# Embedding products in the token selection, and another order for the first expert pair, in an fp32 two-block decoder

## The chip, the cores and the metric

One core of one Trainium2 chip runs the whole program in one launch. The time is in device microseconds (us), the median of three runs. Names: PE is the matrix engine (TensorE; PEld its weight loads), DVE the vector engine, ACT the scalar engine, POOL the general one (GpSimd); SP issues every DMA here and issues them in the order of its queue.

## What is computed

The inputs are one sequence of 512 tokens with 1024 channels, all fp32. A first block (a recurrent mixer, sparse attention, two gated convolution FFNs) is followed by a second one of two layers. Each of these layers has four mixer branches, then an expert-choice MoE with 16 experts, then a gated embedding; the change is in the last two:

```
affinity = softmax((h @ w_router), axis=-1)                  # h = rms_norm(x, g_moe[i])
top_aff, idx = top_k(swapaxes(affinity, 1, 2), 64)           # each expert takes its 64 best tokens
xe = h[idx]
hid = silu(xe @ w_gate_e) * (xe @ w_up_e)                    # 1024 -> 1024, for each expert
ye = hid @ w_down_e
x = x + scatter_add(idx, ye * top_aff)
x = x + sigmoid(rms_norm(x, g_ple[i]) @ w_ple_gate[i]) * (p[i] @ w_ple[i])
```

The products p[i] @ w_ple[i] need no result of the layer: p is an input of 512 tokens by 256 channels, the result has 1024 channels by 512 tokens (2.1 MB).

## The kernel before, in words

Activations stand with channels on the 128 partitions: hT is 8 tiles of [128, 512]. Dense products split both operands into a rounded part and a rest (xh, xl; wh, wl) and take three matmuls per 128x128 block (L408 to L410). Dense weights come as a stream of 512 KB chunks of eight blocks (class Stream): a load into one of four wraw buffers, a rounded copy on ACT (wh), a subtraction on DVE (wl), each into a pool of three buffers.

**The experts** are worked on in eight pairs. Their weights are not split: 384 chunks of 512 KB a layer, 32 for the two up products of a pair and 16 for its down product, each used once by pairmm (L1884: two fp32 matmuls, one per expert, 64 tokens each, which the trace shows as four records). `expert_chunks` is a generator that issues the loads: chunk i goes into the next free buffer, and `chunk()` hands the chunks to PE in the order of the list `order`. There are 36 buffers to begin with: a ring of 21 (11 of its own, the four wraw buffers, three wh and three wl) that is refilled as PE gives buffers back, and 15 that are lent by tiles which are needed only later (hid, yh, yl, hidT, D, xe, sqt, xd) and hold one chunk each, once. `extra` says which chunks go to the lent ones: numbers 2, 5, 8, ... 44. The first loads are issued by `prefetch` in the output projection (`mixer_out`), the rest at the head of `moe`.

**The selection** (the first half of `moe`): PE transposes the router's logits, DVE and ACT make the softmax, PE transposes it to 16 rows of 512 tokens, and DVE takes eight rounds of the eight largest and their replacement (L1839, L1840). A scan counts the chosen tokens along each row (L1844), PE transposes the counts, and DVE compares them with 1 to 64, which gives the one-hot matrix D (L1855). Beside it PE transposes the hidden state, ACT scales and rounds it (xn, xh, L1832, L1833) and POOL makes the rest (L1834).

**The experts' loop:** `gather(q)` picks the tokens of four experts by matmuls with D (L1866, L1867; four steps of 16 matmuls, each giving two of the eight channel tiles of xe). The first one is a generator: `up(0, ahead)` runs a step of it ahead of every second chunk. Then, for p = 0 to 7: up(p + 1); gather(p/2 + 1) when p is even; in the last two rounds also half of the embedding products (`ple_proj`, eight outputs of two blocks, results kept in SBUF as pb); down(p), which combines two pairs into hT when p is odd.

The builder's scheduler orders each engine's instructions by their dependences; what stands in a row is quoted below from the built program.

Of the kernel before, what the change touches and what calls it, by code (L numbers as in the profile page):

```python
# [19 lines left out]
P = 128  # L20
# [172 lines left out]
class Stream:  # L193
    def __init__(self, kb, n_chunks):
        self.kb, self.nch, self.specs, self.pos, self.next, self.ahead = kb, n_chunks, [], CHB, 0, []
        self.pool = False
# [9 lines left out]
    def open(self):  # L206
        kb = self.kb
        if not self.ahead:
            self.preload()
        raw = self.ahead.pop(0)  # L210
        self.h = kb.wsp.tile([P, CHB, P], F32R, name="wh")
        self.l = kb.wsp.tile([P, CHB, P], F32R, name="wl")
        kb.nc.scalar.activation(self.h, raw, AF.Copy)  # L213
        (kb.nc.gpsimd if self.pool else kb.nc.vector).tensor_sub(self.l, raw, self.h.bitcast(F32))  # L214
        self.pos = 0
# [37 lines left out]
class Kern:  # L253
# [773 lines left out]
    def build(self, only2=False):  # L1027
# [18 lines left out]
        with ExitStack() as es:  # L1046
# [3 lines left out]
            for l in range(2):  # L1050
                with ExitStack() as es2:
# [16 lines left out]
                    with ExitStack() as es4:  # L1068
# [5 lines left out]
                        with ExitStack() as es3:  # L1074
                            self.psum_pools(es3, psum)
                            self.mixer_out(l)
                            self.ws.flush()
# [139 lines left out]
    def mixer_out(self, l):  # L1217
# [17 lines left out]
        for d in range(KD):  # L1235
# [12 lines left out]
            self.prefetch(2)  # L1248
        self.stats1()
        route(KD - 1)  # L1250
        self.lg = self.mo2.tile([NE, S], F32, name="lg", tag="sg")
        nc.scalar.activation(self.lg, lg[:NE], AF.Copy)

    def expert_chunks(self, l):
# [3 lines left out]
        order = up(0)  # L1258
# [3 lines left out]

        def ep():
            return self.eraw.tile([P, 2, S], F32, name="eraw")

        def lent():
            for pl, tag, k in ((self.mo2, "hid", 2), (self.mo3, "yh", 3), (self.mo3, "yl", 3), (self.mo1, "hidT", 1),
                               (self.mo2, "D", 1)):
                for _ in range(k):
                    yield pl.tile([P, 2, S], F32, name="raw", tag=tag)  # L1270
            two = self.mid.tile([P, 4, S], F32, name="raw", tag="xe")
            yield two[:, 0:2]
            yield two[:, 2:4]

        def stream():
            for _ in range(4):
                yield self.wraw.tile([P, 2, S], F32, name="wraw")
            for nm in ("wh", "wl"):
                for _ in range(3):
                    yield self.wsp.tile([P, 2, S], F32, name="raw", tag=nm)  # L1280
# [6 lines left out]
        extra = [2 + 3 * j for j in range(15)]  # L1287
        rest = iter([i for i in range(len(order)) if i not in extra])
        for _ in range(NEX):
            load(next(rest), ep())  # L1290
            yield
        for i, raw in zip(extra, lent()):
            load(i, raw)
            yield
        for raw in stream():
            load(next(rest), raw)
            yield
        load(extra[12], self.sqt)
        yield
        for i in extra[13:]:  # L1300
            load(i, self.mo2.tile([P, 2, S], F32, name="raw", tag="xd"))
            yield
        while True:
            for g in ((ep() for _ in range(NEX)), stream()):
                for raw in g:
                    i = next(rest, None)
                    if i is None:
                        return
                    load(i, raw)
                    yield  # L1310
# [481 lines left out]
    def moe(self, l):  # L1792
        nc = self.nc
        keep, two, three = self.mo1, self.mo2, self.mo3
        if True:
            self.prefetch(23 + NEX - len(self.eready))
            posm = self.sq[:NE]
            pT = keep.tile([P, T, NE], F32, name="pT")
            aff = keep.tile([P, T, NE], F32, name="aff")
            bc = lambda a: a[:, :, None].to_broadcast([P, T, NE])  # L1800
            t3 = lambda a: a.rearrange("p (t e) -> p t e", t=T)

            pt = self.pst.tile([P, S], F32, name="t")
# [10 lines left out]
            nc.vector.tensor_tensor(out=aff, in0=aff, in1=bc(sm), op=OP.mult)  # L1814
            pt = self.pst.tile([P, S], F32, name="t")
# [5 lines left out]
            xnh = self.xh.rearrange("p k s -> p (k s)").rearrange("p (t c) -> p t c", t=T)  # L1821
            xnl = self.xl.rearrange("p k s -> p (k s)").rearrange("p (t c) -> p t c", t=T)
            for t in range(T):
                xn = two.tile([P, 2, S], F32, name="xn", tag="xd")
                for hf in range(2):
                    pt = self.mm.tile([P, S], F32, name="mm")
                    for q in range(4):
                        nc.tensor.transpose(pt[:, q * P:(q + 1) * P], self.hT[:, hf * 4 + q, t * P:(t + 1) * P],
                                            self.ident)
                    sl = slice(hf * S, (hf + 1) * S)  # L1830
# [233 lines left out]
```

## Time and profile before

| | us |
|---|---|
| median of 3 runs (lowest, highest) | 3582.73 (3582.24, 3585.94) |
| the profiled execution, its own time | 3584.79 |
| its span | 3583.0 |
| PE busy | 3446.6 (96%) |
| DVE, ACT, POOL busy | 1720.5, 1259.5, 460.5 |
| mean DMA rate over the span | 173 GB/s |

The profiled execution is one run; 1.8 us of its time lie outside the span, and it is 2.1 us above the median. Matmuls overlap in PE's pipeline, so a record is longer than the time to the next one, and a busy PE is not one at its peak. The two MoE stages lie at about 1934 to 2450 and 3009 to 3525 us of the span.

### The profile page before, as it was taken

The page shows a single profiled execution, that of the slowest core. Times are in us where ns is not written, and L with a number is a line of the kernel's source. Part 1 is how long each engine was busy: PE and PEld are TensorE (multiplying, and loading weights), DVE is VectorE, ACT ScalarE, POOL GpSimd, SP SyncE. Part 2 cuts the span into 40 slices and gives each one's busy share as a digit, 9 for nine tenths or more (in the row PEclk, how much of TensorE's full clock was granted, in tenths as well). Part 3 has the DMA queues.
Part 4 walks back from the last instruction along what each step waited for, and adds up shares of the span by engine and source line. Part 5 has one row for each costly group of instructions (what it writes and reads, how often), then busy time and mean ns, then how long its engine had stood idle before and what let it go on. Part 6 is the DMA issues. An engine that isn't in the chain of part 4 may idle for free.

```text
span 3583.0 us, 42155 instructions
## 1 busy us (share of the span) xinstructions
PE 3446.6 (96%) x16156; PEld 2332.3 (65%) x16156; DVE 1720.5 (48%) x3181; ACT 1259.5 (35%) x2207; POOL 460.5 (13%) x356
## 2 busy tenths in 40 slices
PE   7899999999999999999997999999999997999997
PEld 5787888866578888876885433337876885433335
DVE  7745354477765354766664111016666664111015
ACT  5533233366643234435533100014435533100013
POOL 4211011022021012110012000002110012000002
PEclk9999999999999999999999999999999999999999
DMA  3233322311022223221253899994221253999993
GB/s 116 82 107 124 99 95 97 114 39 39 19 83 94 100 95 112 77 71 59 86 189 135 354 419 419 420 391 160 77 71 59 86 188 135 351 419 419 419 391 117
DMA packets 171474, 620.54 MB, mean 173 GB/s; under 512 B 19332, under 2 KB 19588, under 8 KB 171016
## 3 DMA queue, kind: packets, MB, share of 16 engines
q1 hardware_dynamic: 171272, 617.84, 46.0%
q8 instruction: 127, 2.08, 0.2%
q14 instruction: 75, 0.61, 0.1%
HBM read 613.82 MB, written 3.95 MB: 172 GB/s over the span
## 4 chain that ended last, share of the span: by engine, by line
PE 82%; DVE 9%; DMA 4%; ACT 2%; issue 1%; POOL 1%; DVEq 0%; SPq 0%; ACTq 0%; POOLq 0%
PE mm L408 15%; PE mm L409 15%; PE mm L410 15%; PE mm L1884 10%; PE o L1884 5%; DMA eraw<-in_exw 2%; PE o L856 1%; DMA raw<-in_exw 1%; PE mm L1866 1%; PE t L840 1%; DVE wl L214 1%; PE mm L1867 1%; PE o L1585 1%; DVE xl L326 1%; PE o L1724 1%
## 5 line engine op out<-in xcount | busy, mean ns | idle before, releaser
L408 PE MATMUL mm<-xh,wh 128*128 128x512 f32 (+1 forms) x1936 | 767.8, 397 | 6.2 <-DVE mu L1173 4.7
L410 PE MATMUL mm<-xh,wl 128*128 128x512 f32 (+1 forms) x1936 | 761.8, 394 | 2.9 <-DVE wl L214 2.3
L409 PE MATMUL mm<-xl,wh 128*128 128x512 f32 (+1 forms) x1936 | 761.5, 393 | 0.0
L214 DVE TENSOR_TENSOR wl<-wraw,wh 128x1024 fp32r<-128x1024 f32 x356 | 446.3, 1254 | 382.0 <-ACT wh L213 376.6
L213 ACT ACTIVATE wh<-wraw 128x1024 fp32r<-128x1024 f32 x378 | 399.8, 1058 | 585.0 <-PE mm L409 417.8
L408 PEld LDWEIGHTS mm<-xh,wh 128*128 128x128 f32 (+1 forms) x1936 | 364.0, 188 | 94.8 <-issue 6.8
L410 PEld LDWEIGHTS mm<-xh,wl 128*128 128x128 f32 (+1 forms) x1936 | 363.7, 188 | 86.4 <-issue 5.8
L409 PEld LDWEIGHTS mm<-xl,wh 128*128 128x128 f32 (+1 forms) x1936 | 363.9, 188 | 82.2 <-issue 8.2
L341 POOL TENSOR_TENSOR sq<-sq,sqt 128x512 f32<-128x512 f32 x63 | 90.7, 1439 | 1284.3 <-ACT sqt L338 1276.9
L1884 PE MATMUL mm<-eraw,xe 128*64 128x512 f32 x1024 | 248.1, 598 | 1.0 <-DMA eraw<-in_exw 0.9
L1900 DVE TENSOR_TENSOR hid<-sg,mm 128x512 f32<-128x512 f32 x32 | 22.0, 687 | 380.6 <-PE mm L1884 365.9
L1884 PE MATMUL mm<-raw,xe 128*64 128x512 f32 x640 | 159.6, 600 | 1.7 <-DMA raw<-in_exw 1.3
L1884 PEld LDWEIGHTS mm<-eraw,xe 128*64 128x64 f32 x1024 | 70.9, 137 | 136.8 <-issue 108.4
L579 POOL TENSOR_TENSOR fc<-fc,RB 128x512 f32<-128x512 f32 x48 | 85.4, 1779 | 575.7 <-ACT fc L578 575.7
L410 PE MATMUL mm<-gh,wl 128*128 128x512 f32 x384 | 149.5, 389 | 0.0
L408 PE MATMUL mm<-gh,wh 128*128 128x512 f32 x384 | 149.5, 389 | 0.0
L409 PE MATMUL mm<-gl,wh 128*128 128x512 f32 x384 | 149.5, 389 | 0.0
L1174 POOL TENSOR_TENSOR mg<-mg,mu 128x512 f32<-128x512 f32 x48 | 69.5, 1449 | 563.3 <-DVE mu L1173 517.2
L1884 PE MATMUL o<-eraw,hidT 128*64 128x512 f32 x560 | 138.1, 601 | 2.0 <-DMA eraw<-in_exw 0.9
L1899 ACT ACTIVATE sg<-mm 128x512 f32<-128x512 f32 x32 | 19.1, 597 | 312.4 <-PE mm L1884 312.4
L1926 ACT ACTIVATE yh<-o,af 128x512 fp32r<-128x512 f32 x32 | 22.0, 687 | 293.6 <-PE o L1884 293.4
L1927 DVE SCALAR_TENSOR_TENSOR yl<-o,af,yh 128x512 fp32r<-128x512 f32 x32 | 24.0, 750 | 189.3 <-ACT yh L1926 189.1
(492 smaller groups left out, 5704.8 us busy)
## 6 DMA issues: line engine op xcount, KB each, us to landing
eraw<-in_exw SPq DMA_DIRECT2D x396, 512.0 KB, 9.9
wraw<-in_wst SPq DMA_DIRECT2D x378, 512.0 KB, 3.3
raw<-in_exw SPq DMA_DIRECT2D x232, 512.0 KB, 9.9
wraw<-in_exw SPq DMA_DIRECT2D x138, 512.0 KB, 9.9
tb<-t5d SPq DMA_DIRECT2D x8, 448.0 KB, 3.4
mixt<-in_mix SPq DMA_DIRECT2D x2, 1344.0 KB, 6.3
hT<-in_xT SPq DMA_DIRECT2D x8, 256.0 KB, 6.0
out_dram<-po SPq DMA_DIRECT2D x8, 256.0 KB, 2.3
```

Source lines behind the costliest of these rows:

```text
L213: kb.nc.scalar.activation(self.h, raw, AF.Copy)
L214: (kb.nc.gpsimd if self.pool else kb.nc.vector).tensor_sub(self.l, raw, self.h.bitcast(F32))
L326: nc.vector.scalar_tensor_tensor(self.xl[:, k, :], h, g, self.xh[:, k, :].bitcast(F32), op0=OP.mult, op1=OP.subtract)
L341: nc.gpsimd.tensor_add(acc, acc, t)
L408: nc.tensor.matmul(out, a, h, start=(k == 0), stop=False)
L409: nc.tensor.matmul(out, a, l, start=False, stop=False)
L410: nc.tensor.matmul(out, b, h, start=False, stop=(k == n - 1))
L579: nc.gpsimd.tensor_mul(c0, c0, self.RB)
L840: nc.tensor.transpose(pt[:, r * P:(r + 1) * P], srcs(i, r), self.ident)
L856: nc.tensor.matmul(o[0][c % 2 * HD:(c % 2 + 1) * HD], lhs(i), pe, start=(c < 2), stop=False)
L1174: nc.gpsimd.tensor_add(m, m, u)
L1884: nc.tensor.matmul(ps[e * CAP:(e + 1) * CAP], x[:, k, off + e * CAP:off + (e + 1) * CAP], raw[:, e], start=(k == 0), stop=(k == KD - 1))
```

## The change

Six edits, the same in both layers:

1. `ple_load` and `ple_proj` are called in `mixer_out` and between the steps of the selection, no longer in rounds 6 and 7. The results go through two-tile buffers of the wraw pool (pbs) to DRAM (pbd) in four stores, and `ple` reads them back in two loads. pT and the two chunks of w_ple are loaded in the output projection; `preopen` splits three chunks ahead of their use.
2. The scan is replaced: the last round's values are transposed, compared (mk), and a matmul with a triangular matrix (`tri`, a new input) plus three with a column of ones give the running count. The first round reads PSUM directly. posm, the row form that `combine` needs, is made by PE transposes after the first pair.
3. D of the first gather is made in three pieces.
4. The first pair has k outermost: `up_first` holds four accumulators, and a step of the gather is followed by eight chunks.
5. Lent buffers hold chunks 8, 11, ... 50; loads are issued in another order (21 in the output projection, 15 in the selection).
6. down(p) comes before the gather of the next four experts.

```diff
 class Stream:
...
+    def preopen(self):
...
+        h = kb.wsp.tile([P, CHB, P], F32R, name="wh")
+        l = kb.wsp.tile([P, CHB, P], F32R, name="wl")
+        kb.nc.scalar.activation(h, raw, AF.Copy)
+        (kb.nc.gpsimd if self.pool else kb.nc.vector).tensor_sub(l, raw, h.bitcast(F32))
+        self.opened.append((h, l))
...
@@ mixer_out
+            if d == 2:
+                self.ple_load(l)
+            for _ in range(max(d - KD + 3, 0) and KD - d):
+                self.ws.preopen()
+            self.prefetch(3 if d < 5 else 2)
...
+        sums(0, self.sq)
+        (wh, wl, r), = self.ws.take([("w_router_2", l, (KD - 1) * P, (0, NE))])
+        self.ple_proj(l, 0, pre[0], (0, 1))
...
+        self.ple_proj(l, 0, pre[0], (1, 2))
+        self.ple_proj(l, 1, pre[1])
@@ expert_chunks
-        order = up(0)
+        order = [(0, q * KD + 2 * k2 + i) for k2 in range(KD // 2) for q in range(4) for i in range(2)]
...
-        extra = [2 + 3 * j for j in range(15)]
+        extra = [8 + 3 * j for j in range(15)]
...
+        late = ("wh", "wl", "sqt", "wh", "wl", "r", "r", "r", "xd", "xd", "wh", "wl", "hidT", "D", "r")
@@ moe
+            turn(0)
+            po = lambda: self.pso.tile([P, S], F32, name="o")
+            self.ple_proj(l, 2, po())
...
-            w = [two.tile([NE, S], F32, name="sg") for i in range(2)]
-            nc.vector.tensor_copy(w[0], pt[:NE])
...
-            nc.vector.tensor_scalar(w[1], w[0], -1e29, None, op0=OP.is_le)
-            nc.vector.tensor_tensor_scan(posm, on, w[1], 0.0, op0=OP.mult, op1=OP.add)
-            nc.vector.tensor_mul(posm, posm, w[1])
...
+            nc.vector.tensor_scalar(mk, t3(pt[:, :T * NE]), -1e29, None, op0=OP.is_le)
+            pc = self.pst.tile([P, S], F32, name="t")
+            nc.tensor.matmul(pc[:, :T * NE], tri, mk.rearrange("p t e -> p (t e)"), start=True, stop=False)
+            for t in range(T - 1):
+                nc.tensor.matmul(pc[:, (t + 1) * NE:T * NE], one,
+                                 mk[:, t:t + 1].to_broadcast([P, T - 1 - t, NE]), start=False, stop=(t == T - 2))
+            nc.vector.tensor_tensor(out=pT, in0=t3(pc[:, :T * NE]), in1=mk.bitcast(F32), op=OP.mult)
...
+            def up_first(ahead):
+                pp = [self.psum() for _ in range(4)]
+                for k2 in range(KD // 2):
+                    next(ahead)
+                    for ps in pp:
+                        for k in range(2 * k2, 2 * k2 + 2):
+                            pairmm(ps, XE[0], 0, self.chunk(), k)
...
                 if p + 1 < NPAIR:
                     up(p + 1)
+                down(p)
                 if p % 2 == 0 and p // 2 + 1 < 4:
                     for _ in gather(p // 2 + 1):
                         pass
-                if p >= NPAIR - 2:
-                    half = p - (NPAIR - 2)
-                    if half == 0:
-                        self.ple_load(l)
-                    self.ple_proj(l, half)
-                down(p)
...
     def ple_proj
+        if d % 2 == 0:
+            self.pbs = self.wraw.tile([P, 2, S], F32, name="pbs", tag="wraw")
+        nc.scalar.activation(self.pbs[:, d % 2], ps, AF.Copy)
+        if d % 2:
+            nc.sync.dma_start(self.pbd[:, d - 1:d + 1], self.pbs)
...
     def ple(self, l):
+            self.pb = [self.mid.tile([P, KD // 2, S], F32, name="pb", tag="xe") for _ in range(2)]
+            for i, pb in enumerate(self.pb):
+                nc.sync.dma_start(pb, self.pbd[:, i * KD // 2:(i + 1) * KD // 2])
```

The order on PE in the selection of layer 1, before (lg are the logits, aff the affinities, hT the hidden state; each x counts matmuls):

```order
L1828 MATMUL mm<-ident,hT 128x128 x6
L1805 MATMUL t<-ident,lg 128x16 x4
L1828 MATMUL mm<-ident,hT 128x128 x18
L1817 MATMUL t<-ident,aff 16x128 x4
L1828 MATMUL mm<-ident,hT 128x128 x8
```

and in the changed program at the same place (ph, pl are the split p):

```order
L1860 MATMUL t<-ident,lg 128x16 x4
L1845 MATMUL mm<-ident,hT 128x128 x8
L416 MATMUL o<-pl,wh 128x512
L417 MATMUL o<-ph,wl 128x512
L1845 MATMUL mm<-ident,hT 128x128 x8
L1877 MATMUL t<-ident,aff 16x128 x4
L415 MATMUL o<-ph,wh 128x512
```

Embedding products now stand ahead of and behind the transposes of the affinities, and 16 of the hidden state's transposes still stand ahead of them.

The order on PE in the first expert pair of layer 1, before (eraw and raw are loaded chunks, D the one-hot matrix; the chunk's x counts two matmuls a chunk, and L1884 alone is one of the two):

```order
L1884 MATMUL mm<-eraw,xe 64x512
L1866 MATMUL mm<-D,xh 128x256
L1867 MATMUL mm<-D,xl 128x256
L1866 MATMUL mm<-D,xh 128x256
L1867 MATMUL mm<-D,xl 128x256
L1866 MATMUL mm<-D,xh 128x256
L1867 MATMUL mm<-D,xl 128x256
L1866 MATMUL mm<-D,xh 128x256
L1867 MATMUL mm<-D,xl 128x256
L1884 MATMUL mm<-eraw,xe 64x512 x3
```

and in the changed program:

```order
L1946 MATMUL mm<-eraw,xe 64x512 x16
L1928 MATMUL o<-D,xh 128x256
L1929 MATMUL o<-D,xl 128x256
L1928 MATMUL o<-D,xh 128x256
L1929 MATMUL o<-D,xl 128x256
L1928 MATMUL o<-D,xh 128x256
L1929 MATMUL o<-D,xl 128x256
L1928 MATMUL o<-D,xh 128x256
L1929 MATMUL o<-D,xl 128x256
L1946 MATMUL mm<-raw,xe 64x512 x2
L1946 MATMUL mm<-eraw,xe 64x512 x4
```

Eight chunks stand between pieces of the gather where one or two stood.

The order in SP's queue at the end of the expert stage of layer 1, before (in_exw are expert weights, in_wst the weight stream, in_pT the embeddings):

```order
L1284 DMA eraw<-in_exw 128x1024
L1977 DMA pt<-in_pT 128x1024
L202 DMA wraw<-in_wst 128x1024
L1284 DMA eraw<-in_exw 128x1024 x10
L1284 DMA wraw<-in_exw 128x1024 x4
L1284 DMA raw<-in_exw 128x1024 x2
L202 DMA wraw<-in_wst 128x1024
L1284 DMA eraw<-in_exw 128x1024 x2
```

and in the changed program:

```order
L1296 DMA eraw<-in_exw 128x1024 x11
L1296 DMA raw<-in_exw 128x1024
L203 DMA wraw<-in_wst 128x1024 x2
L2076 DMA pb<-pbd 128x2048 x2
L203 DMA wraw<-in_wst 128x1024 x12
```

The three loads for the embedding products have left the expert loads, and the read back stands behind the first two chunks of the next weights.

## Rows read from the trace of the kernel before

**Rows 1.** The page: the chain that ended last, share of the span by engine.
```profile
PE 82%; DVE 9%; DMA 4%; ACT 2%; issue 1%; POOL 1%; DVEq 0%; SPq 0%; ACTq 0%; POOLq 0%
```

**Rows 2.** Stretches: us, PE, PEld, DVE, ACT, POOL busy (x), PEclk, DMA, GB/s.
```profile
1940.00:1950.00 10.00, 0.86 (x7) 0.46 (x5) 9.51 (x22) 5.69 (x11) 8.40 (x7) 0.65 0.20 66
1964.50:2000.00 35.50, 35.50 (x172) 14.90 (x172) 3.33 (x5) 4.37 (x7) 0.00 (x0) 1.00 0.73 270
2030.00:2050.00 20.00, 19.29 (x123) 11.89 (x123) 2.96 (x5) 4.28 (x9) 0.00 (x0) 1.00 0.80 313
2050.00:2390.00 340.00, 332.50 (x1466) 120.14 (x1464) 44.38 (x65) 29.57 (x50) 0.00 (x0) 1.00 1.03 419
2390.00:2420.00 30.00, 29.03 (x116) 12.24 (x118) 4.82 (x6) 5.79 (x9) 0.00 (x0) 0.94 0.85 335
1956.80:2435.00 478.20, 469.02 (x2113) 182.30 (x2114) 65.36 (x94) 54.14 (x93) 3.81 (x3) 0.99 0.96 389
```

**Rows 3.** Timeline of PE, layer 1: start us, us, what, [idle before <-releaser].
```profile
1954.52 0.61 PE L1848 MATMUL t<-ident,sq 16*128 16x16 f32 x4 [13.66 <-DVE sq L1845]
1956.80 0.55 PE L1866 MATMUL mm<-D,xh 128*128 128x256 f32 x1 [1.67 <-DVE D L1855]
...
1961.26 1.07 PE L1884 MATMUL mm<-eraw,xe 128*64 128x512 f32 x2
```

**Rows 4.** Timeline of PE: expert products in one run, and the stage's last.
```profile
1991.25 7.89 PE L1884 MATMUL mm<-raw,xe 128*64 128x512 f32 x36
...
2433.34 1.44 PE L1884 MATMUL o<-wraw,hidT 128*64 128x512 f32 x3
```

**Rows 5.** Timeline of SP's queue, layer 1: issues of loads.
```profile
1964.51 22.13 SPq L1284 DMA_DIRECT2D eraw<-in_exw  x11
...
2371.63 0.33 SPq L1977 DMA_DIRECT2D pt<-in_pT  x1
...
2399.60 0.33 SPq L202 DMA_DIRECT2D wraw<-in_wst  x1
...
2413.67 0.80 SPq L1284 DMA_DIRECT2D raw<-in_exw  x2
...
2418.37 0.47 SPq L1284 DMA_DIRECT2D wraw<-in_exw  x1
```

**Rows 6.** Waits of SP's queue, 1860 to 2450: total, times, longest us.
```profile
SPq L1284 <- PE o L1884: 22.3, 37, 9.5
```

**Rows 7.** Timeline of PE: the embedding products, both runs, and what follows each.
```profile
2384.22 0.50 PE L408 MATMUL mm<-ph,wh 128*128 128x512 f32 x1 [1.33 <-ACT wh L213]
...
2389.89 0.65 PE L1884 MATMUL o<-eraw,hidT 128*64 128x512 f32 x2
...
2406.53 0.50 PE L408 MATMUL mm<-ph,wh 128*128 128x512 f32 x1
...
2413.80 0.65 PE L1884 MATMUL o<-raw,hidT 128*64 128x512 f32 x2
```

**Rows 8.** Lines of ACT, 1934 to 1960; and tile pb: ns least, median, most.
```profile
L1832 ACT ACTIVATE xn<-mm,rstd 128x512 f32<-128x512 f32 x8 | 5.1, 684 | 1.7 <-DVE rstd L355 1.6
...
L1990 ACT ACTIVATE pb<-mm x16: 597/598/600, 2386.8 to 3489.5; 128x512 f32<-128x512 f32 x16
```

**Rows 9.** Timeline of DVE, layer 1: the end of the selection.
```profile
1939.38 0.68 DVE L1819 COPY sg<-t 16x512 f32<-16x512 f32 x1 [0.70 <-PE t L1817]
...
1952.54 1.21 DVE L1844 TENSOR_TENSOR_SCAN sq<-RB,sg 16x512 f32<-16x512 f32 x1
1953.79 0.68 DVE L1845 TENSOR_TENSOR sq<-sq,sg 16x512 f32<-16x512 f32 x1
...
1955.43 1.22 DVE L1855 TENSOR_TENSOR D<-pT,cst2t 128x1024 fp32r<-128x1024 f32 x1
```

**Rows 10.** Layer 2: PE's last expert product, and a stretch as in rows 2.
```profile
3508.96 1.44 PE L1884 MATMUL o<-wraw,hidT 128*64 128x512 f32 x3
...
3465.00:3495.00 30.00, 29.03 (x117) 12.27 (x117) 4.83 (x6) 5.79 (x9) 0.00 (x0) 0.94 0.84 330
```

More of the change, by code (lines that the diff above doesn't have):

```diff
@@ L1261, in expert_chunks @@
         order += down(NPAIR - 1)
[L1263 to L1280, printed above, removed]
+        extra = [8 + 3 * j for j in range(15)]
+        rest = iter([i for i in range(len(order)) if i not in extra])
+        lent = iter(extra)
         def load(i, raw):
@@ L1285, in load, with ring @@
             self.eready[i] = raw
-        extra = [2 + 3 * j for j in range(15)]
-        rest = iter([i for i in range(len(order)) if i not in extra])
+        def ring(tag):
+            i = next(rest, None)
+            if i is None:
+                return
+            if tag == "e":
+                load(i, self.eraw.tile([P, 2, S], F32, name="eraw"))
+            elif tag == "r":
+                load(i, self.wraw.tile([P, 2, S], F32, name="wraw"))
+            else:
+                load(i, self.wsp.tile([P, 2, S], F32, name="raw", tag=tag))
@@ L1289, in expert_chunks, with lend @@
+        def lend(pl, tag):
+            load(next(lent), pl.tile([P, 2, S], F32, name="raw", tag=tag))
         for _ in range(NEX):
-            load(next(rest), ep())
+            ring("e")
             yield
-        for i, raw in zip(extra, lent()):
-            load(i, raw)
-            yield
[L1295 to L1301, printed above, removed]
+        for pl, tag, k in ((self.mo2, "hid", 2), (self.mo3, "yh", 3), (self.mo3, "yl", 3)):
+            for _ in range(k):
+                lend(pl, tag)
+                yield
@@ new lines, in expert_chunks @@
+        two = self.mid.tile([P, 4, S], F32, name="raw", tag="xe")
+        for b in range(2):
+            load(next(lent), two[:, 2 * b:2 * b + 2])
+            yield
+        late = ("wh", "wl", "sqt", "wh", "wl", "r", "r", "r", "xd", "xd", "wh", "wl", "hidT", "D", "r")
+        for tag in late:
+            if tag == "sqt":
+                load(next(lent), self.sqt)
+            elif tag == "hidT":
+                lend(self.mo1, tag)
+            elif tag in ("xd", "D"):
+                lend(self.mo2, tag)
+            else:
+                ring(tag)
@@ L1302, in expert_chunks @@
             yield
         while True:
[L1304 to L1310, printed above, removed]
+            for tag in ("e",) * NEX + tuple(t for t in late if t in ("wh", "wl", "r")):
+                n = len(self.eready)
+                ring(tag)
+                if len(self.eready) == n:
+                    return
+                yield
@@ L1956, in moe @@
             ahead = gather(0)
-            next(ahead)
-            up(0, ahead)
+            up_first(ahead)
             for _ in ahead:
                 pass
+            pt = self.pst.tile([P, S], F32, name="t")
+            for t in range(T):
+                nc.tensor.transpose(pt[:NE, t * P:(t + 1) * P], pT[:, t], self.ident)
+            nc.vector.tensor_copy(posm, pt[:NE])
             for p in range(NPAIR):
```

138 lines of the change are left out of this document (88 added, 50 removed).

## The prediction

> **What bounds the kernel now.** The page's chain comes first: PE holds 82% of it, DVE 9%, DMA 4% [rows 1], so a microsecond counts where PE waits or where its last product is set. The stretches of layer 1 come next [rows 2]. In the expert stage, 1956.8 to 2435, PE is busy 469 of 478 us, and DMA runs at 419 GB/s for 340 us on end, a level that it does not pass. An expert load is 512 KB: 1.25 us at 419 GB/s. On PE a load is four records, and 36 records (nine loads) take 7.9 us [rows 4]: 0.88 us a load. PE eats faster than DMA feeds, and only its other work (gathers, transposes, combining) keeps the two close.
>
> So I count loads in SP's queue [rows 5]. Of the 384 expert loads of a layer 36 stand ready; the first refill is issued at 1964.5, the last expert load at 2418.4. Between lie 348 refills and three loads for the embedding products (pT and two weight chunks): 351 x 1.25 = 439 us, ending at 2403. Three stretches fall short of 419 GB/s [rows 2]: 1964.5 to 2000 loses 35.5 x (1 - 270/419) = 12.6 us, 2030 to 2050 5.1, 2390 to 2420 6.0, together 23.7. That gives 2427, and PE's last expert product ends at 2434.8 [rows 4], 8 us behind. The sum meets the trace, so I use it as the model: end = start of the refills + loads x 1.25 + lost + 8.
>
> What loses them: at the start PE eats six loads in 16 us between gather products, and loads 2 and 5 lie in lent buffers, which are not refilled. At 2030 the gather for the next four experts stands between up(1) and down(0): nothing is eaten and the ring is full. At 2390 the split embedding weights sit in slots of the weight pools that later loads need; SP waits 9.5 us for PE [rows 6] and goes on at 2413.67, when the second run of products ends [rows 5, 7]. Before all this PE stands idle 13.66 us for the selection and 1.67 for the one-hot matrix [rows 3].
>
> **The products leave the stage.** Their two runs take 2384.2 to 2389.9 and 2406.5 to 2413.8, with a wait of 1.3 before the first [rows 7]: 14.3 us of PE per layer. By the model this is no gain in itself; what goes is the three loads, 3.8 us, and the stop at 2390, 6.0 (bounds 3 and 6: something else may fill the ring there).
>
> **The selection.** The 48 products, at most those 13 us, go into PE's gap of 13.66 and cost nothing while DVE's eight rounds run. If that cover were gone they would cost those 13 us. DVE loses the copy (0.68), the scan and the product after it (1.21, 0.68), and waits for a quarter of the one-hot comparison (0.3) in place of 1.22 [rows 9]: 3.5 us. It gains two small operations and four matmuls, which the trace does not have: four 16-column transposes take 0.61 [rows 3], so I take 1.0 with hand-overs (0.5 to 2). Against this, PE now has about a dozen product matmuls and 16 transposes ahead of the transposes of the affinities, and ACT has eight evictions of 0.60 (4.8 us) among the eight xn copies (5.1 us) [rows 8]: 0 to 5 us, I take 1.5. Net 1 us earlier (between 3 earlier and 4 later): the first gather product at 1956. Splitting pT and its two weight chunks moves into the output projection, where a block of PE's work covers a chunk's split; a late chunk would show as a gap there, at 1 to 2 us each.
>
> **The stores.** Four of 512 KB, 5 us of DMA in all, fall where DMA moves 66 GB/s [rows 2]; I cost them at nothing. But SP is in order: behind the last store stand seven expert loads, and it waits for ACT's last eviction. ACT's work from 1937 on (5.1, about as much for xh, 4.8) ends near 1952; eight transfers then keep DMA busy to 1962. By then refills are due: 24 gather products precede the first expert product where there were 32 in 4.5 us [rows 3], so PE eats from 1959 to 1961. The queue therefore runs full from 1962, 2.5 us before the 1964.5 of now (bounds 1959 and 1967).
>
> **First pair, k outermost.** A gather step of 16 products (2 us) is followed by eight loads (7 us). Of the first 32 loads eight are lent now (numbers 8, 11 and on), so 24 slots come free in some 36 us, or 30 us of DMA from 1962: 4 us lost in place of 12.6 (bounds 2 and 10). Its four accumulators are evicted by ACT and DVE while PE finishes the later ones; no wait follows.
>
> **Gather after down.** down(0) now frees 16 slots (20 us of DMA) before the 10 us gather: 1 us lost in place of 5.1 (0 to 5).
>
> **The read back.** Two loads of 1 MB, 5 us, follow the last expert load and two weight chunks. The third chunk waits behind them, but PE has 16 blocks of three matmuls first, 11 us. I take 0; the bound is 5 a layer.
>
> **Sum for a layer.** -2.5 (earlier start), -3.8 (three loads), -8.6 (start), -4.1 (gather), -6.0 (stop) = -25. By the model the end is 1962 + 435 + 5 + 8 = 2410 against 2434.8. Layer 2 shows the same (last product at 3510.4; 330 GB/s in the stretch that answers to 2390 [rows 10]), so -50 in all. The profiled execution took 3584.8 (span 3583.0); its time less 50 is 3535. The median of the runs is 2 us lower, so 3534 is within what its sum can tell.
>
> **The rivals.** (1) *PE binds, not the loads.* Then a layer gains what PE sheds: 14.3 and 1 in the chain, say 15, and the time is 3555. For it: PE busy 98% of the stage. Against it: the flat 419 GB/s, and 0.88 us a load when fed. The Trainium skill ("Perfetto Trace Analysis", section Identifying the Most-Contended Engine) says that matmul busy share is not a good measure of headroom, since pipelined instructions overlap in it, and that weight-load busy time is. Here that is 182 us of 478 [rows 2], so by that rule the slack is PE's and the sum above stands; by the busy row it is 3555. The trace agrees with the rule.
>
> (2) *The queue fills at once.* Refills from 1959, 2 us lost at the start, and a tail of 5 us: 31 a layer, 3523. Nothing in the trace excludes it; it needs every bound at its good end.
>
> (3) *The lost stretches only move.* The ring fills again at other pauses, and only the three loads go: 7.5 us in all, 3577. For it: 21 ring slots hold 26 us of DMA, no more. Against it: each stretch has a cause that the change removes.
>
> (4) *Slower: SP's queue stops at the stores.* A store waits for ACT, its buffer is a ring slot that comes back only when it has landed, and the seven loads and all refills stand behind the last one. Each us that it is late after 1952 costs one. At 1977 the gain is gone; at 1982 the kernel is 10 us slower, 3595. For it: both waits are new. Against it: ACT has 15 us of work there, not 45.
>
> That the change does not do what it says is excluded by the order of the built program, quoted above.
>
> **How the numbers follow.** A measurement of this kernel can tell 0.2%, 7 us, from no change. The forecast (3523 to 3546) has 0.63, rival 1 0.15, rival 2 0.13, rival 3 0.04, rival 4 0.03; 0.02 is left for no change by causes that cancel. Faster than 0.2%: 0.63 + 0.15 + 0.13 + 0.03 of rival 3, whose 7.5 is on the edge: 0.94. Same: 0.03. Slower: 0.03. The range, 3514 to 3560, takes in rivals 1 and 2 and the bounds of the start and of the read back, and leaves out 3 and 4.
>
> **What would show it.** Right: the last refill-bound stretch at 419 GB/s begins near 1962 and has no dip near 2390; the first expert product comes at 1959 to 1961; the gap of 13.66 us holds products; PE's last expert product of layer 1 comes near 2410; SP waits for PE less than 5 us after 2300. Wrong: the rate stays below 400 after 1985; PE's waits for loads vanish altogether (then PE binds, rival 1); SP stands before a store past 1960 (rival 4); DVE's product with pb waits for a load (the read back is exposed).

## The result, and the profile after

The changed kernel takes 3558.64 us (median of 4 runs, 3555.74 to 3560.38), the kernel before 3582.84 in the runs beside it: ratio 0.9927, interval 0.9916 to 0.9939. The forecast was 3534: the gain is 24 us where 49 were expected. The time lies in the range, near its upper edge, and the case that was held likeliest (3523 to 3546) did not come. The edge was there for rival 1 and for wide bounds of the start and the read back; rival 1 is not what happened (below). The profiled execution has a span of 3557.6, 25.4 below that of before.

The page's chain that ended last, in shares of the span, looks like [rows 1], so it tells nothing yet:

```profile
PE 82%; DVE 8%; DMA 5%; ACT 2%; issue 1%; POOL 1%; DVEq 0%; SPq 0%; ACTq 0%; POOLq 0%
```

Stretches of layer 1 in the changed kernel, columns as in [rows 2]; the first is the expert stage from its first expert product to its last:

```profile
1960.40:2419.30 458.90, 451.47 (x2043) 165.84 (x2042) 61.83 (x91) 44.33 (x78) 4.25 (x3) 1.00 1.01 409
1955.00:1962.00 7.00, 7.00 (x32) 5.68 (x33) 0.00 (x0) 1.42 (x3) 0.00 (x0) 0.51 1.02 410
1962.20:2000.00 37.80, 37.80 (x198) 16.19 (x196) 3.66 (x6) 4.85 (x8) 0.00 (x0) 1.00 0.90 336
2000.00:2050.00 50.00, 50.00 (x262) 22.33 (x258) 5.08 (x8) 6.25 (x12) 0.00 (x0) 1.00 1.02 414
2050.00:2100.00 50.00, 49.72 (x216) 16.77 (x216) 8.22 (x11) 2.95 (x5) 0.00 (x0) 1.00 0.99 392
2100.00:2390.00 290.00, 284.32 (x1267) 101.69 (x1263) 34.98 (x53) 23.19 (x41) 0.00 (x0) 1.00 1.03 419
2390.00:2410.00 20.00, 18.53 (x69) 4.92 (x69) 4.98 (x7) 2.58 (x5) 0.00 (x0) 1.00 1.03 419
```

The stage is 458.9 us long where it was 473.5 (1961.3 to 2434.8), in layer 2 458.3 where it was 473.9. The dip at 2390 is gone (419 GB/s). The start moves 336 GB/s in place of 270, and a loss has come in 2050 to 2100, where the kernel before ran at 419: by the forecast's own count 7.5 us are lost in 1962 to 2000, 0.6 to 2050, 3.2 to 2100, 11.3 in all against the 5 that were forecast (4 at the start, 1 at the gather). Of the forecast's signs, the dip is gone and SP waits for PE 4.0 us after 2300; the rate is still 300 GB/s in 1985 to 2000 and 410 behind that.

The timeline of PE in the changed kernel: the selection's gaps and the stage's first and last expert product.

```profile
1951.08 0.41 PE L1901 MATMUL t<-ident,sg 16*128 16x16 f32 x4 [3.14 <-DVE sg L1897]
1951.81 0.42 PE L1904 MATMUL t<-cum 128*128 128x64 f32 x1 [0.32 <-DVE cum L1902]
1952.05 0.79 PE L1906 MATMUL t<-cum 128*128 128x48 f32 x3
1953.70 0.55 PE L1928 MATMUL o<-D,xh 128*128 128x256 f32 x1 [0.87 <-DVE D L1917]
...
1960.37 1.12 PE L1946 MATMUL mm<-eraw,xe 128*64 128x512 f32 x2
...
2418.29 1.03 PE L1946 MATMUL o<-raw,hidT 128*64 128x512 f32 x4
```

PE's gap of 13.66 [rows 3] holds the products and is down to 3.14; the first gather product comes at 1953.7, 3.1 us earlier than before, the first expert product at 1960.4, only 0.9 earlier: 24 of the gather's matmuls and six of `t<-aff,D` stand between the two, and PE does them at half of its clock (0.51 in 1955 to 1962; 0.64 in the same 7 us of the kernel before, whose lower level ends at 1960.0). The last comes at 2419.3, 15.5 us earlier; 25 were forecast.

Not all of these 3.1 and 0.9 us come from the selection. The output projection's last product, before and changed:

```profile
1930.30 0.39 PE L410 MATMUL mm<-xh,wl 128*128 128x512 f32 x1
```

```profile
1928.66 0.39 PE L417 MATMUL mm<-xh,wl 128*128 128x512 f32 x1
```

It starts 1.6 us earlier, and in e3, e9 and e10, which are the kernel before up to there, it starts at 1928.7, 1927.1 and 1929.7: executions differ by that much. Counted from it, the first gather product comes 1.5 us earlier (25.0 in place of 26.5) and the first expert product 0.7 later (31.7 in place of 31.0); in layer 2 the latter is 30.8 in place of 30.9. The shorter selection is used up by the time that the first expert product stands behind it.

The timeline of SP's queue in the changed kernel. Counting its issues (36 loads stand ready, so the first row begins with the 37th, number 36 counted from 0), the third row holds loads 99 to 109, the fifth 114 to 116, the last two 372 to 383:

```profile
1962.20 11.92 SPq L1296 DMA_DIRECT2D eraw<-in_exw  x11
...
2018.64 10.93 SPq L1296 DMA_DIRECT2D eraw<-in_exw  x11
...
2042.97 16.97 SPq L1296 DMA_DIRECT2D eraw<-in_exw  x11
2061.99 5.87 SPq L1296 DMA_DIRECT2D raw<-in_exw  x4
2069.20 2.04 SPq L1296 DMA_DIRECT2D wraw<-in_exw  x3
...
2388.89 13.19 SPq L1296 DMA_DIRECT2D eraw<-in_exw  x11
2402.98 0.33 SPq L1296 DMA_DIRECT2D raw<-in_exw  x1
```

The refills begin at 1962.2, as forecast. Eleven of them take 10.9 us at 2018, but 17.0 at 2043: the ring is full there, PE is in the gather for the next four experts (to 2050.7), and the queue waits for its products. Its waits in 2040 to 2075 (total, times, longest us):

```profile
SPq L1296 <- PE mm L1946: 19.8, 19, 6.3
```

The last load is issued at 2403.0 (2418.4 before) and PE's last expert product ends 16.3 us behind it (16.4 before). So what came earlier came through the loads, but fewer microseconds of it than the sum had.

Waits of SP's queue, changed kernel, 1860 to 2450, for [rows 6] and for the stores:

```profile
SPq L1296 <- PE o L1946: 15.8, 29, 1.5
...
SPq L2067 <- ACT pbs L2065: 6.3, 4, 3.1
```

The wait of 9.5 for `o` is gone (1.5 at most). It was not the one at 2390, as the forecast read it: it lies in 2030 to 2050, at the first later gather, ahead of load 85. The stop that ends at 2413.67 is the longest in another row of the kernel before, 9.0 us for an embedding product, which is gone too:

```profile
SPq L1284 <- PE mm L410: 16.1, 4, 9.0
```

The four stores wait 6.3 us together, the last is issued at 1949.0 and all loads behind it by 1956: the rival of a queue held up by the stores did not come. The read back holds nobody: among PE's waits of 2420 to 2480 the longest is the 1.3 us for `pg` that the kernel before has there too.

### The profile page after: what moved, and what is told of

It reads as the page before. It is cut to its first block, busy times and chain, and to the rows that moved or that the text cites. A ratio compares the mean times of both kernels' runs of the same rounds, so it can differ in the third digit from the quotient of the medians.

```text
span 3557.6 us, 42279 instructions
## 1 busy us (share of the span) xinstructions
PE 3449.5 (97%) x16172; PEld 2331.6 (66%) x16172; DVE 1716.1 (48%) x3181; ACT 1259.2 (35%) x2211; POOL 458.8 (13%) x354
## 4 chain that ended last, share of the span: by engine, by line
PE 82%; DVE 8%; DMA 5%; ACT 2%; issue 1%; POOL 1%; DVEq 0%; SPq 0%; ACTq 0%; POOLq 0%
PE mm L415 15%; PE mm L416 15%; PE mm L417 15%; PE mm L1946 11%; PE o L1946 4%; DMA eraw<-in_exw 3%; PE o L863 1%; PE t L847 1%; DMA raw<-in_exw 1%; DVE wl L215 1%; PE mm L1928 1%; PE o L1616 1%; PE o L1755 1%; PE t L1498 1%; DVE xl L333 1%
```

## The experiments

All were run beside the kernel before; ratios are to it. In the table a stage is counted from its first expert product (t = 0) in layer 1: when loads 57, 85, 101, 114, 200 and 383 (the last) are issued and when the last expert product ends, all in us, counted from the issues and products in each trace. Layer 2 agrees within 1.7 us in each kernel. The medians of the kernel before beside them were 3582.8 to 3585.9.

| kernel | median us | ratio, interval | 57 | 85 | 101 | 114 | 200 | 383 | end |
|---|---|---|---|---|---|---|---|---|---|
| before | 3582.8 | | 38.8 | 79.9 | 94.4 | 111.8 | 219.2 | 457.1 | 473.5 |
| changed | 3558.6 | 0.9927, 0.9916 to 0.9939 | 33.4 | 66.0 | 91.4 | 108.8 | 214.1 | 442.6 | 459.0 |
| e3, before, no products | 3582.3 | 0.9991, 0.9982 to 1.0 | 38.8 | 79.9 | 94.7 | 111.9 | 219.7 | 454.4 | 470.5 |
| e4, changed, no products | 3553.3 | 0.9908, 0.9887 to 0.9929 | 33.7 | 66.7 | 91.2 | 102.6 | 214.3 | 441.5 | 458.0 |
| e5, lent early | 3562.3 | 0.9937, 0.9921 to 0.9953 | 36.3 | 67.2 | 91.7 | 109.1 | 214.4 | 442.3 | 459.1 |
| e6, first pair old | 3562.8 | 0.9937, 0.9922 to 0.9951 | 33.4 | 66.7 | 92.1 | 109.5 | 214.8 | 443.1 | 459.8 |
| e7, gather before down | 3567.0 | 0.9947, 0.9928 to 0.9967 | 33.5 | 77.2 | 93.4 | 109.6 | 216.9 | 446.8 | 463.5 |
| e8, lent late | 3559.9 | 0.9929, 0.9914 to 0.9944 | 30.8 | 61.7 | 91.6 | 109.1 | 214.3 | 442.7 | 459.4 |
| e9, before, down first | 3576.3 | 0.9983, 0.9974 to 0.9993 | 38.8 | 69.5 | 93.4 | 108.5 | 216.4 | 453.8 | 470.3 |
| e10, before, no embedding | 3573.8 | 0.9975, 0.9966 to 0.9984 | 38.8 | 79.9 | 94.4 | 111.9 | 219.3 | 449.1 | 465.9 |
| e11, gather spread | 3571.1 | 0.9966, 0.9954 to 0.9979 | 33.4 | 80.9 | 96.0 | 112.1 | 220.6 | 450.4 | 467.2 |
| e12, spread, lent late | 3568.7 | 0.9955, 0.9942 to 0.9967 | 30.8 | 71.1 | 94.6 | 110.5 | 217.4 | 446.8 | 463.5 |

### Do the loads bind, or PE? (e1 to e4)

In e1 and e2 the two kernels load half of every block:

```
-            nc.sync.dma_start(raw.rearrange("p b c -> p (b c)"), self.aps["exw"][(l * NPAIR + p) * 6 * KD + r])
+            nc.sync.dma_start(raw[:, 0], self.aps["exw"][(l * NPAIR + p) * 6 * KD + r][:, :S])
...
-                    nc.tensor.matmul(ps[e * CAP:(e + 1) * CAP], x[:, k, off + e * CAP:off + (e + 1) * CAP], raw[:, e],
+                    nc.tensor.matmul(ps[e * CAP:(e + 1) * CAP], x[:, k, off + e * CAP:off + (e + 1) * CAP], raw[:, 0],
```

> The changed kernel with each expert load cut to its first half (256 KB: one of the two experts; PE multiplies by that half twice, so its work is the same). Theory M (mixed): in a layer PE stands behind the loads only in one stretch, some 21 loads paced at 1.25 us where PE takes 0.86, 8 us a layer, and the last 26 us are PE's own; with loads that are never late these 8 us go, twice: 3542 (3538 to 3547). Theory P (PE binds from end to end): PE had no load to wait for, 3558 within 4. Theory L (loads bind everywhere, the forecast's model): the end follows the loads down until PE's own work binds, below 3540.

> The same cut in the kernel before, whose PE waits at two stretches (some 16 and 5 loads at 1.25 us where PE takes 0.86): M says 8 us a layer, 3567 (3562 to 3571), so that the two kernels with half loads differ by the products and little else, 25 to 29 us. P says 3583. L says below 3560, with the difference to the changed kernel gone down to PE's 14 us a layer.

Measured: 3493.98 (ratio 0.9742, 0.9724 to 0.9759) and 3521.78 (0.9819, 0.9798 to 0.9839): 65 and 63 us less than with whole loads. P falls; the loads bind in both kernels. M had its size wrong by a factor of four. The two differ by 27.8 us: with loads that are hardly ever late (0.5 us of waits for them in a layer at most), the 14 us of products in each layer count in full.

Why M was wrong is seen on PE. The timeline of the changed kernel where it does wait for loads, and behind that where it does not:

```profile
2367.45 1.08 PE L1946 MATMUL mm<-wraw,xe 128*64 128x512 f32 x4 [0.17 <-DMA wraw<-in_exw]
2368.74 1.08 PE L1946 MATMUL mm<-raw,xe 128*64 128x512 f32 x4 [0.22 <-DMA raw<-in_exw]
...
2394.42 1.08 PE L1946 MATMUL o<-wraw,hidT 128*64 128x512 f32 x4 [0.79 <-DVE hidT L1988]
2395.43 1.07 PE L2014 MATMUL t<-sq,ident 16*64 16x512 f32 x2
2396.43 1.08 PE L1946 MATMUL o<-raw,hidT 128*64 128x512 f32 x4
2397.44 1.07 PE L2014 MATMUL t<-sq,ident 16*64 16x512 f32 x4
```

and the same work in e1:

```profile
2372.31 6.18 PE L1946 MATMUL o<-eraw,hidT 128*64 128x512 f32 x28
2378.42 1.93 PE L2014 MATMUL t<-sq,ident 16*64 16x512 f32 x8
```

From 2367 to 2394 one load follows the other at 1.25 us, PE taking 0.86: the 8 us of M, of which the stage's rows record 4.0 as waits for loads. But the order of PE's program itself is another in e1. With whole loads single loads and combining work alternate, with half loads each comes in one run: eight `t<-sq,ident` take 1.93 us in one run, and 1.07 for two where they are split. Counted in the traces, the expert products of a layer stand in 89 runs in the changed kernel and in 35 in e1; within a run a product starts 0.217 us behind the one before it, at a run's end 0.52 go by to the next matmul. Summed from start to start, the expert products take 14.9 us less in e1, which these 54 run ends explain (54 x 0.3); the `t<-DT` pairs, which start 0.34 and 0.30 apart in place of 0.26 each, take 8.1 less, `t<-sq,ident` 4.6 and the gathers 2.8: 30.4 of the 31.0 us (458.9 to 427.9). So e1 and e2 show that loads bind, but not by how much PE waits, since the order changed with them.

e3 and e4 leave the products out (the cut is e3's; e4 also leaves out the evictions, the stores and the read back):

```
-            self.dense(ps, [("w_ple_2", l, k * P, d * P) for k in range(2)], self.ph, self.pl)
-            nc.scalar.activation(pb[:, d % 4], ps, AF.Copy)
+            self.ws.take([("w_ple_2", l, k * P, d * P) for k in range(2)])
+            nc.scalar.activation(pb[:, d % 4], self.RB, AF.Copy)
```

> The kernel before without the 48 products of the embedding in each layer (the three loads, the splits and eight evictions of 0.6 us stay; the results are replaced by a constant row). P: PE sheds 13 to 14 us a layer, 3555. L: only the stop at the weight slots goes, 6 us a layer, 3571. M: the arrival of load 368 moves by that stop, and PE's last 26 us follow it: 7 us a layer, 3569 (3565 to 3573).

> The changed kernel without the products, their evictions, the four stores and the read back (the weights are still loaded and split; the embedding term is replaced by a constant row). The forecast's terms say that all of it is covered: 3558 within 4. Rival S: the products, the evictions or the queue of stores delay the selection or the refills, and the read back delays the third gate chunk: 4 to 6 us a layer, 3547 to 3551.

e3: 3582.29, no faster to speak of (0.9991, 0.9982 to 1.0); its stages are 3.0 and 3.8 us shorter, with 3.4 us more of each at the lower clock level, which costs up to 1.7. So 13 us of PE's work in each layer were worth 3 to 5.5 us: rival 1 of the forecast (PE binds, 3555), whose figure is nearest to the measured time, is not what happened. L and M expected 6 and 7. Its queue shows what they had missed:

```profile
2390.47 1.56 SPq L1284 DMA_DIRECT2D raw<-in_exw  x2
2396.56 0.33 SPq L202 DMA_DIRECT2D wraw<-in_wst  x1
2396.94 1.45 SPq L1284 DMA_DIRECT2D eraw<-in_exw  x2
2401.63 5.35 SPq L1284 DMA_DIRECT2D raw<-in_exw  x4
```

The second chunk of embedding weights still stands in the queue for its slot, 4.5 us behind the loads ahead of it (2390.47 + 1.56 to 2396.56), and the queue stops again at 2398.4, for 3.2 us, while the split weights keep theirs. The stop hangs on the three loads and the slots as much as on the products. e4: 3553.31 (0.9908, 0.9887 to 0.9929), between the forecast's figure and rival S's; the interval overlaps the changed kernel's. Its stages are 458.0 and 458.4 long: the products, stores and read back cost the stage 1.0 us in layer 1 and nothing in layer 2. They cost the selection more. The output projection's last product in e4, the first gather product and the first expert product:

```profile
1926.10 0.39 PE L417 MATMUL mm<-xh,wl 128*128 128x512 f32 x1
...
1950.47 0.58 PE L1928 MATMUL o<-D,xh 128*128 128x256 f32 x1 [0.78 <-DVE D L1917]
...
1955.46 5.00 PE L1946 MATMUL mm<-eraw,xe 128*64 128x512 f32 x22
```

Behind the projection, the gather comes at 24.4 us (25.0 with the products) and the first expert product at 29.4 (31.7); in layer 2 0.9 and 1.7 us earlier. The six `t<-aff,D` no longer stand ahead of it in e4, so part of this is order. Together that is 4.0 us, of the 5.3 by which the medians differ.

### What was the start worth? (e5, e6, e8)

e5 puts `extra` back to `2 + 3 * j`; e8 spreads the lent buffers (the cut below); e6 is the old order of the first pair (`order = up(0)`, and `next(ahead)` before each second of its loads):

```
-        extra = [8 + 3 * j for j in range(15)]
+        extra = [8, 13, 33, 58, 63, 38, 68, 73, 18, 23, 78, 48, 53, 28, 43]
```

> The changed kernel with the lent buffers at loads 2, 5, 8 and on as before, in place of 8, 11, 14 and on. L (the loads set the end; the last product follows the last load issued by 16 us, as in the kernel before, the changed one and the one without products): fewer slots come back in the first 16 us, 2 to 5 us of DMA lost again in each layer, 3563 to 3569. If the place of the lent buffers doesn't matter (the first pair's order alone filled the queue): 3558 within 3.

> The changed kernel with the first pair's products in the old order (six loads between the gather's steps, then the rest), lent buffers still at 8, 11 and on. L: the loss at the start, 8 us now, goes back toward the 12.6 of the kernel before: 3563 to 3569. Rival: with loads 2 and 5 no longer lent, the old order frees slots as fast: 3558 within 3.

> The changed kernel with the fifteen lent buffers spread over loads 8, 13, 18 to 78 in place of 8, 11 to 50, each as late as its owner allows. L: slots come back faster than the 1.25 us of a load, the 11 us that are lost now after the first refill go down to 3 to 6, and the end follows: 5 to 8 us a layer, 3543 to 3549. M (PE's own last 26 us and the products bind): at most 2 us a layer, 3555 to 3558.

e5: 3562.28, e6: 3562.78, e8: 3559.89. The total times can't tell them from the changed kernel (all intervals overlap); the stages are 459.1, 459.8 and 459.4 long against 459.0, and show none of the 2 to 8 us a layer that L had. e8 does at first what it should. The timeline of its SP queue, loads 78 to 88, 99 to 109 and 114 to 116:

```profile
2012.96 13.25 SPq L1296 DMA_DIRECT2D eraw<-in_exw  x11
...
2040.33 19.34 SPq L1296 DMA_DIRECT2D eraw<-in_exw  x11
...
2068.92 2.04 SPq L1296 DMA_DIRECT2D wraw<-in_exw  x3
```

Load 57 comes 2.6 us earlier in the stage than in the changed kernel, load 85 4.3 us; and by load 101 all is gone (91.6 against 91.4). e5 is 2.9 late at load 57 and 0.3 at load 101. Where the ring is full, the next load goes out when PE has read one, whatever the queue gained before. Up to about load 114 (at 108 to 110 us in all of these) PE sets the queue, through the gathers and the combining, in which it reads no loads. (At load 200 the queue waits for PE once more, but DMA runs on at 418 to 420 GB/s there, so nothing is lost.) The losses at the start are not lost to the end: they only move. The stretches from the first refill to 40 us into the stage and from 90 to 125, in e5, the changed kernel and e8:

```profile
1963.70:2001.70 38.00, 38.00 (x198) 16.25 (x196) 3.66 (x6) 4.85 (x8) 0.00 (x0) 1.00 0.85 300
2051.70:2086.70 35.00, 35.00 (x156) 11.53 (x156) 4.47 (x6) 2.27 (x4) 0.00 (x0) 1.00 1.02 411
```

```profile
1962.20:2000.40 38.20, 38.20 (x198) 16.30 (x196) 3.66 (x6) 4.85 (x8) 0.00 (x0) 1.00 0.90 336
2050.40:2085.40 35.00, 35.00 (x155) 11.31 (x156) 4.78 (x6) 2.27 (x4) 0.00 (x0) 1.00 0.97 380
```

```profile
1961.70:1999.90 38.20, 38.20 (x200) 16.30 (x198) 3.65 (x6) 4.85 (x8) 0.00 (x0) 1.00 0.96 357
2049.90:2084.90 35.00, 35.00 (x155) 11.43 (x156) 4.56 (x6) 2.27 (x4) 0.00 (x0) 1.00 0.91 349
```

Counted against 419 GB/s they lose 10.8, 7.6 and 5.7 us in the first stretch, and 0.7, 3.3 and 5.8 in the second. Rival 3 of the forecast said this of all of the change and had 0.04; for the start it is what happened.

### Gather after down (e7, e9), and the embedding (e10)

```
-                down(p)
                 if p % 2 == 0 and p // 2 + 1 < 4:
                     for _ in gather(p // 2 + 1):
                         pass
+                down(p)
```

> The changed kernel with the next four experts' gather before down(p) again. L: the loss in the stretch of the first such gather goes from 3.2 back to 5.1 a layer, 2 us each: 3562 (3559 to 3565). Rival: the order of gather and down does nothing: 3558 within 2.

> The kernel before with one line moved: down(p) ahead of the gather, as in the change. Theory R (the last full ring sets the clock): time that the loads lose early is lost for the end only if no later full ring waits for PE; in the kernel before the queue stops last for the embedding's slots, at load 374 of 384, 15 us behind a run of loads without a stop from load 120 on, so an earlier gain of 4 to 5 us in a layer is all given back there: 3583 (3580 to 3586). Theory L (losses add up, the forecast's sum): 4.1 us a layer, 3575 (3573 to 3577).

> The kernel before without the embedding's loads, splits, products and evictions in the last rounds (its term replaced by a constant row): what the change takes out of the stage, with nothing put elsewhere. R: the stop at the end is gone, the last full ring is the one at load 85, 80 us into the stage, and from there the loads run through as in the changed kernel with the gather before down: 7 us a layer, 3568 (3565 to 3572). L: the three loads and the stop, 9.8 us a layer, 3563. PE binds: 14 to 16 us a layer, 3552.

e7: 3567.01 (0.9947, 0.9928 to 0.9967, which still overlaps the changed kernel's interval); its stages are 4.5 and 5.5 us longer than the changed kernel's, where L had 2. Its SP timeline, loads 78 to 88:

```profile
2020.65 21.67 SPq L1296 DMA_DIRECT2D eraw<-in_exw  x11
```

and its waits in 2025 to 2045:

```profile
SPq L1296 <- PE o L1946: 14.8, 7, 12.1
```

With the gather ahead of down the queue stands 12.1 us before load 85, and from there the loads run through: 298 x 1.25 = 372.5 would bring the last at 449.7, it comes at 446.8 (the loads held back go out faster at first). With down ahead, PE frees 16 slots before the gather, load 85 goes out at 66.0, and the full ring comes at load 114, at 108.8; 269 x 1.25 = 336.3 from there gives 445.1, measured 442.6. e10 and e11 have their last full ring at load 85 too, at 79.9 and 80.9, and end 2.4 and 3.7 later than e7, as those times are later. So the time of the **last full ring** that stops DMA sets the end, to within some 3 us by this count.

e9 is R's miss. R expected nothing, since the kernel before stops at load 374 afterwards; 3576.25 came (0.9983, 0.9974 to 0.9993), L's figure, and 3.2 us a stage. The queue of e9 still stops at load 374, but at 449.1 in the stage in place of 452.4: what it waits for are PE's products, and PE had been waiting for loads ahead of them, so earlier loads bring the products earlier as well. Of the 4.6 us that the gather's stretch loses less (0.5 in place of 5.1), the stop takes back 1.8 (7.7 in place of 5.9). A later stop only swallows an early gain if PE reaches it at the same time anyway.

e10, with nothing of the embedding in the stage: 3573.75 (0.9975, 0.9966 to 0.9984); stages of 465.9 and 466.1, 7.6 and 7.8 us shorter. R had 7, L 9.8. The total time lies above R's range (3565 to 3572): 3.6 us more go by between the stages than before (below).

### Can it be had better? (e11, e12)

```
-                    up(p + 1)
+                    q = p // 2 + 1 if p % 2 == 0 and p // 2 + 1 < 4 else 0
+                    up(p + 1, gather(q) if q else iter(()))
                 down(p)
-                if p % 2 == 0 and p // 2 + 1 < 4:
-                    for _ in gather(p // 2 + 1):
-                        pass
...
                         pp.append(ps)
+                        next(ahead, None)
```

> The changed kernel with the four steps of each later gather put one by one behind the quarters of up(p+1), in place of one run behind down(p); lent buffers still every third load from 8, in another order of owners. R: the ring no longer fills at the gathers (load 114 at 108 us, load 200 at 214 us into the stage), and the next full ring, 2 to 4 us earlier on the same line, takes over: 2 to 4 us a layer, 3551 to 3555. If PE's own work binds in that stretch, no change: 3558.

> The same with the lent buffers at every fifth load from 8 to 78. R: now that no full ring follows, the early losses count, and this order takes them away as well: with the loads running through from the first refill a layer ends 435 us + 16 us behind it, 5 to 6 us earlier than now, 3547 (3545 to 3552); alone the late lent buffers gave nothing. If it is no better than the spread gather alone, R's account of the early losses is wrong.

Both are slower than the changed kernel: 3571.14 and 3568.71 (0.9966 and 0.9955). Spreading put the gather ahead of down again: at load 85 PE had read 65 loads at 80.9 us, as in the kernel before (65 at 79.9). The expectation had left out the 16 slots that down frees first. With the lent buffers late on top (e12) the stage is 3.7 us shorter than in e11, while the same move alone gave nothing (e8). The ring is full until the same moment, 80.9 us, with 65 loads read in both, but in e12 it is load 88 that goes out then, not load 85: three of the lent buffers (numbers 68, 73 and 78 in the order of use) are still unread, so three more of the loads read so far gave a ring slot back, and 3 x 1.25 = 3.75. In e8 the last stop of DMA comes at load 101, with 81 loads read and every lent buffer behind PE. R's sentence that no full ring would follow is not what happened. No version that was run beats the changed kernel.

## Why the prediction was right and wrong

By its own steps, for a stage of layer 1, against what the runs put in their place (the last three are differences of stage lengths in the table, taken in this order, and add up to the 14.5 between 473.5 and 459.0; e7 against e10 holds all that edits 2 to 5 do in the stage, and gather after down alone, e9, gives 3.2):

| step | forecast | measured | from |
|---|---|---|---|
| earlier start | -2.5 | -0.9 | first expert product 1961.3 to 1960.4, the projection ahead of it 1.6 earlier |
| three loads and the stop at 2390 | -9.8 | -7.6 | e10 against before |
| losses at the start | -8.6 | -2.4 | e7 against e10 |
| gather after down | -4.1 | -4.5 | changed kernel against e7 |
| sum | -25 | -15.4 | 15.5 in the trace |

**The model** was right in its kind: loads at 1.25 us and a fixed distance from the last load issued to the last product (16.1 to 16.8 us in layer 1 in all these kernels but the half-load ones) carry the stage, and PE's 13 us of products are worth little by themselves (e3). The Trainium skill's rule that the forecast leaned on ("Perfetto Trace Analysis", section Identifying the Most-Contended Engine: the busy share of matmuls is not a good measure of how close a kernel is to its limit) agrees with the trace: PE is busy 98% of the stage, and halving the loads takes 31.0 us from it, part of it by another order.

**The step that failed** is the sum of the lost stretches. They were taken as independent of each other, as if a microsecond saved at the start were saved at the end. That holds behind the last full ring only. Ahead of it the ring fills anyway and the queue waits for PE; the start's 8.6 us were worth 2.4 while the gather stood ahead of down, and about 1 after it was moved (e6, 459.8 against 459.0). In the forecast's own terms, read from the rates of the changed kernel: the start still loses 7.5 us in place of 12.6 (4 were forecast), the gather 3.8 in place of 5.1 (1), and the last product ends 11 us behind the loads by this count, not 8, a distance that was taken as fixed. With -2.3 at the start of the refills, -3.8 for the three loads and -6.0 for the stop that is -15.5. 7.5 and 3.8 lie inside the bounds that the forecast gave these two terms. Which step this was could be read from [rows 2]: a loss in 2030 to 2050 that follows the one of 1964 to 2000 means that the ring was full again by then, so the first loss had been made up.

**The refills' start** came at 1962.2 as forecast, with some luck: the queue is tied to PE's first expert product, and that came 0.9 earlier only because the projection ended 1.6 earlier in this execution. The rest is the first pair's order: the first refill follows 1.8 us behind that product in place of 3.3. Gather after down is worth 4.5 in the stage, near its 4.1, though its own stretch saves 1.3. The stores and the read back were hidden, as costed. The products were hidden but for 0.7 to 0.9 us at the first gather product (e4), where 1.5 was taken; the selection came out 1.5 us shorter to the gather, where 1 was forecast. What the forecast had wrong there is the way from the gather to the first expert product: it put 24 gather products there, and six `t<-aff,D` at the lower clock level stand there too, so it takes 6.7 us in place of 4.5 [rows 3]. The stop at 2390 was sized right by the rates (6.0), but from a wait that lies elsewhere (9.5 for 9.0). In the stage it gave less: e10 gains 7.6 where the three loads and the stop are 9.8, since there, too, the last product ends farther behind the loads; why it does is not shown.

**Outside the stages** 5.7 us were given back: 3.5 between the last expert product of layer 1 and the first of layer 2 (601.7 before, 605.2 after) and 2.2 behind the last of layer 2 (72.6 and 74.8). The first goes with the granted clock. Stretches at its lower level ahead of the selection, changed kernel and then before, columns as above (the last but two is PEclk):

```profile
2548.90:2555.70 6.80, 5.80 (x18) 4.97 (x19) 6.80 (x17) 2.89 (x8) 1.22 (x1) 0.50 0.17 49
2944.90:2948.30 3.40, 3.40 (x10) 2.62 (x9) 1.39 (x2) 0.83 (x2) 1.83 (x1) 0.50 0.68 196
```

```profile
2564.20:2567.60 3.40, 3.03 (x12) 2.77 (x13) 3.40 (x10) 1.74 (x4) 1.22 (x1) 0.50 0.00 0
```

10.2 us at 0.50 in place of 3.4 cost PE up to 3.4 us more. Over the twelve kernels with whole loads that distance is 601.5 to 605.3: 601.5 to 604.2 in the five that spend 3.4 us at the lower level there, 604.1 to 605.3 in the seven that spend 6.8 or 10.2. It follows no part of the change (601.5 in e9, 605.3 in e10, 602.4 in e5, 605.2 in e6), so it is not put down to one. Behind layer 2 the mean clock is 0.87 in place of 0.90, which can make up to 1.8 of the 2.2; no run separates this. What makes the clock fall in some executions stays open. The sum closes: 14.5 + 0.9 and 15.6 in the stages and at their starts, less 5.7, is 25.3, and the span fell by 25.4.

## What to carry to other kernels

Where a ring of buffers stands between a load queue and its reader, a stretch in which the queue moves less than it could is lost to the end, in these runs, only behind the last moment at which the full ring stops DMA: find that moment first (the last long wait of the queue for the reader), count the loads that are out at it, cost everything ahead of it by what it does to the reader, and only what follows by bytes. A start time that moved is read from the last product ahead of the change, not from the start of the execution. Work that is taken off an engine which waits for loads is worth what it frees in slots and loads, not its own duration; and before the reader pauses for something else, let it free slots first.

## What the runs showed that was not expected

- Halving every load took 31 us from a stage in which PE's rows show 4.0 us of waits for loads: most of the difference stands in no wait, but in a program order that alternates single loads with other matmuls. A run's end costs PE 0.3 us here (0.52 from one start to the next in place of 0.217), 89 times a layer.
- The stage's length is steadier than the total time: 459.0, 459.1, 459.8 and 459.4 in four kernels whose medians lie between 3558.6 and 3562.8. Small differences of an order are told by counting loads in the trace, where a total time cannot.
- Selection in the changed kernel: the gather products run at the lower clock level (0.51 in 1955 to 1962, above). PE had been busy up to 1947.9 and idle for 3.14 us up to four short transposes at 1951.1, and the lower level lasts from 1951.6 to 1961.8; in the kernel before, idle for 13.66 us, it lasts from 1943.0 to 1960.0. Filling PE's gap with 13 us of work made the lower stretch shorter, but did not take it off the gather.
